# Projections to the merge gates read their tokens with a step of 2, 4, 8 or 16

## The chip, the core and the metric

The kernel runs on one core of a Trainium2 chip, as one launch. The metric is device time in microseconds from the start to the end of one execution. A profiled execution also gives the span from its first to its last instruction and a record of every instruction on the five engines: PE (TensorE, with its weight loads PEld), DVE (VectorE), ACT (ScalarE), POOL (GpSimd) and SP (SyncE).

## The reference

512 tokens of width 2048 go through two blocks in float32. The part that the change touches is the first block's pair of merge gates, `g_att` and `g_ssm`, each 2048 wide:

```
h = rms_norm(x, ln_gain)                      # 512 x 2048
proj = h @ w_in                               # 512 x 10240
q, k, v, z_att, u, z_ssm, g_att, g_ssm = split(proj)
...                                           # attention on q, k, v; a grouped state-space branch on u
merged = sigmoid(g_att) * (y_att @ w_proj_att) + sigmoid(g_ssm) * (y_ssm @ w_proj_ssm)
x = x + merged @ w_out
```

The second block (two layers of three kinds of attention, each with its projections and a gate) follows and is not touched.

## The kernel before

Activations are held transposed: features on the 128 partitions, the 512 tokens along each partition. The normalised input is 16 tiles `xg`, one per 128 features, of shape 128 x 2 x 512: a high half rounded to fp32r and a low half with the remainder, so that a product takes three fp32r matmuls (`mm3`, L180: high by high, high by low, low by high) that add up in PSUM. Weights come from memory in units of 128 x 1024 (`wunit`, L192), are split in the same way by ACT (L189) and DVE (L190), and wait in three buffers `hl`.

`gemm_t` (L224) makes a product in the transposed layout: the weights are stationary (128 x 128), the tokens stream as the moving operand, 512 columns in a row, and two PSUM tiles `pg` of 128 x 512 are filled over the 16 feature tiles. That is 2 x 16 x 3 = 96 matmuls of 512 columns in one call. PSUM has four `pg` buffers, so that one call's two tiles can be emptied during the next call.

`accumulate` (L246) walks the matmuls of a call, and after each group of three calls `tick`, which takes steps of other work that were pushed beside it. This sets the order: while the gates are computed, the steps of the state-space branch (`ssm`, L482) lie between the groups of three. Among these steps are small fp32 matmuls: L549 (16 columns), L557 and L584 (64 columns side by side), and L586, whose moving operand is `st[:, :64, g0 + q + g]` of a tile of 65 x 64 elements, so 64 columns that stand 64 elements (256 bytes) apart. An fp32 matmul is two records in the trace.

The gates are the loop at L638 to L645: 16 calls of `gemm_t`, eight for `g_att` (columns from GA0) and eight for `g_ssm` (from GS0). After each call, for each of its two PSUM tiles, DVE multiplies by the row `row` of inverse norms into a tile `t` (L643), ACT takes the sigmoid in place (L644), and POOL issues the store to the scratch `sg_d` (L645). Later, at L689 and L690, these are loaded as the merge needs them.

Three DVE operations elsewhere use steps along a partition: L629 reads PSUM and `row` with a step of 8 elements (32 bytes), L559 writes `st` with a step of 64, L708 writes with a step of 8.

Of the kernel before, what the change touches and what calls it, by code (L numbers as in the profile page):

```python
# [17 lines left out]
T = 512  # L18
# [9 lines left out]
Q0, K0, V0, ZA0, U0, ZS0, GA0, GS0 = 0, 1024, 2048, 3072, 4096, 5120, 6144, 8192  # L28
# [89 lines left out]
class Net:  # L118
# [102 lines left out]
                pass  # L221
        self.between = []

    def gemm_t(self, src, c0, mov, n=T):  # L224

        out = [self.psg()[:, :n] for _ in range(2)]

        def step(hl, k, kk, i, first, last):
            x = mov[k]
            c = slice(i * P, (i + 1) * P)  # L230
            self.mm3(out[i], hl[:, 0, kk, c], hl[:, 1, kk, c], x[:, 0], x[:, 1], first, last)

        return self.accumulate(src, c0, len(mov), out, step, AT_MEM if n == NMEM else AT_T)

    def gemm_tok(self, src, c0, mov, nt, cw=256):

        out = [self.psg()[:, :cw] for _ in range(nt)]

        def step(hl, k, kk, i, first, last):
            x = mov[k]  # L240
            t = slice(i * P, (i + 1) * P)
            self.mm3(out[i], x[:, 0, t], x[:, 1, t], hl[:, 0, kk], hl[:, 1, kk], first, last)

        return self.accumulate(src, c0, len(mov), out, step, AT_TOK if cw == 256 else AT_T, cw)
# [350 lines left out]
    def first(self):  # L595
        nc, tc, a = self.nc, self.tc, self.a
        v = nc.vector
        w_in = a["w_in"]
# [8 lines left out]
        with ExitStack() as sx:  # L607
            xp = sx.enter_context(tc.tile_pool(name="xg1", bufs=KD, reuse_waits="tile"))
            xg = []
            by_chunk = "p (m j) -> p j m"  # L610
            with ExitStack() as ix:
                stage = ix.enter_context(tc.tile_pool(name="ins", bufs=2, side="right", reuse_waits="tile"))
                mx = ix.enter_context(tc.tile_pool(name="memx", bufs=KD, side="right", reuse_waits="tile"))
                acc = self.new_acc()
                for _ in self.transposed_in(a["x"], 4, xp, xg, self.ln_g, stage, acc, spill=self.xt_d):
                    pass
                row, cols = self.norm_stats(acc)
                self.row, self.cols = row, cols
                self.more_columns()
                mem, acc = [], stage.tile([P, 512], F32, name="macc", bufs=1)[:, :NMEM]  # L620
                for f in range(0, 8, 2):
                    if f == 4:
                        self.push(self.transposed_in(a["mem"], 2, mx, mem, self.mem_g, stage, acc), MEM_IN_EVERY)
                    us = self.gemm_t(w_in, U0 + f * P, xg)
                    self.ahead = AHEAD
                    for i, ps in enumerate(us):
                        t = self.t512()
                        with self.soon():
                            v.tensor_mul(t.rearrange("p (j m) -> p j m", j=8), ps.rearrange(by_chunk, j=8),  # L629
                                         row.rearrange(by_chunk, j=8))  # L630
                        self.store(self.u_d[(f + i) * P:(f + i + 1) * P], t)
                self.flush()
                self.rpb_windows()
                self.memory_kv(mem, *self.norm_stats(acc, NMEM, stage))
            with tc.tile_pool(name="ssm", bufs=3, side="right", reuse_waits="tile") as sp:

                self.push(self.ssm(sp), SSM_EVERY)
                work = [(c0 + f * P, self.sg_d[s], f) for s, c0 in enumerate((GA0, GS0)) for f in range(0, KD, 2)]  # L638
                for c0, dst, f in work:
                    for i, ps in enumerate(self.gemm_t(w_in, c0, xg)):  # L640
                        t = self.t512()
                        with self.soon():
                            v.tensor_mul(t, ps, row)  # L643
                        nc.scalar.activation(t, t, AF.Sigmoid)  # L644
                        self.store(dst[(f + i) * P:(f + i + 1) * P], t)  # L645
                self.ssm_gates(xg, 0)
                self.flush()
            with tc.tile_pool(name="glu", bufs=8, side="right", reuse_waits="tile") as gp:
                yt, yh = [], []
                self.push(self.ssm_out(gp, yt, yh), GELU_EVERY)  # L650
                self.ssm_gates(xg, 4)
                self.flush()
                for f in range(0, 8, 2):
                    for i, ps in enumerate(self.gemm_t(a["w_glu"], f * P, yh)):
                        t, z = self.t512(), self.t512()
                        r = slice((f + i) * P, (f + i + 1) * P)
                        self.load(z, self.zs_d[r])
                        last = nc.scalar.activation(t, ps, AF.Sigmoid, bias=self.b_glu[:, f + i:f + i + 1])
                        v.tensor_mul(t, t, yt[f + i])
                        v.tensor_mul(z.rearrange(by_chunk, j=8), z.rearrange(by_chunk, j=8),  # L660
                                     t.rearrange("p (j m) -> p j m", j=8))
                        self.store(self.ys_d[r], z)
            self.exp_tables(last)
            with tc.tile_pool(name="att1", bufs=2, side="right", reuse_waits="tile") as ap:
                self.causal = ap.tile([P, 512], F32, name="causal", bufs=1)
                self.load(self.causal, a["causal"])
                for h in range(0, 8, 2):
                    self.diff_heads(ap, h, xg)
                self.flush()
            yp = tc.alloc_tile_pool(name="y1", bufs=16, side="right", reuse_waits="tile")  # L670
            ya, ys = [], []
            for f in range(0, 8, 2):
                for i, ps in enumerate(self.gemm_t(w_in, ZA0 + f * P, xg)):
                    ya.append(self.gated(yp, ps, f + i))
            for f in range(8):
                t = self.t512()
                self.load(t, self.ys_d[f * P:(f + 1) * P])
                h = yp.tile([P, 2, 512], FR, tag="yh", name=self.nm("yh"))
                self.split(h[:, 0], h[:, 1], t)
                ys.append(h)  # L680
        mp = tc.alloc_tile_pool(name="mrg", bufs=KD, side="left", reuse_waits="tile")
        mg = []
        for f in range(0, KD, 2):
            pa = self.gemm_t(a["w_proj_att"], f * P, ya)
            pb = self.gemm_t(a["w_proj_ssm"], f * P, ys)
            for i in range(2):
                r = slice((f + i) * P, (f + i + 1) * P)
                t, u = self.t512(), self.t512()
# [6 lines left out]
                h = mp.tile([P, 2, 512], FR, tag="m", name=self.nm("m"))  # L695
# [4 lines left out]
        xg, acc = [], self.new_acc()  # L700
        self.x1_d = dram.tile([D, T], F32, name="x1_d")
        for f in range(0, KD, 2):
            for i, ps in enumerate(self.gemm_t(a["w_out"], f * P, mg)):
                k = f + i
                r = slice(k * P, (k + 1) * P)
                t, o = self.t512(), self.t512()
# [569 lines left out]
```

## Time and profile before

| | us |
|---|---|
| two runs, median (lowest to highest) | 3308.08 (3307.55 to 3308.61) |
| the profiled execution, whole | 3310.56 |
| its span, first to last instruction | 3308.7 |
| PE busy in the span | 3272.4 (99%) |
| DVE busy | 1749.5 (53%) |
| ACT busy | 1168.2 (35%) |
| first to last L643 (emptying of the gates' tiles) | 231.4 to 630.5 |

The profile gives each engine's busy time, the span in 40 slices with the clock that TensorE was granted, the chain of work that ended last, and groups of instructions by source line with durations and the idle time before them. Matmuls overlap: a record's duration is longer than the distance to the next matmul's start, and its end is modelled. So the pace of PE is read from the starts in a timeline, and what a column costs from the difference of durations between shapes.

### The profile page before, as it was taken

To read this page: it belongs to the slowest core of one execution; us is meant where nothing else is said; L and a number is where in the kernel's file an instruction comes from. 1 tells how busy PE (TensorE), PEld (TensorE's weight loads), DVE (VectorE), ACT (ScalarE), POOL (GpSimd) and SP (SyncE) were. 2 spreads that over 40 slices of the span, in tenths; PEclk is the share of its full clock that TensorE was granted. 3 is DMA by queue.
4 is the path that set the end of the run, shared out by engine and by line. 5 is a ranking of instruction groups with operands and counts; after the bars stand their busy time and mean duration, and the time that the engine had idled before them with its cause. 6 is when DMAs were issued, how large, how long until landed. Compare 5 with 4: busy or idle time off the path is not lost.

```text
span 3308.7 us, 43728 instructions
## 1 busy us (share of the span) xinstructions
PE 3272.4 (99%) x17268; PEld 2794.0 (84%) x17268; DVE 1749.5 (53%) x3207; ACT 1168.2 (35%) x1811; POOL 292.9 (9%) x426
## 2 busy tenths in 40 slices
PE   8999999999999999999999999999999999999998
PEld 6998877888888788888888888888888888888788
DVE  5464486445888754434444556443354445554333
ACT  4432222243555432233333334323333333343322
POOL 3200001311111000011011000001100100000000
PEclk9999999999999999999999999999999999999999
DMA  6564443453333354344333222334443222223433
GB/s 222 181 199 120 128 124 120 136 188 134 98 101 99 109 183 151 124 142 154 96 95 100 90 83 80 121 118 143 147 135 100 95 90 90 83 93 121 144 120 102
DMA packets 359805, 410.03 MB, mean 124 GB/s; under 512 B 36506, under 2 KB 314921, under 8 KB 359472
## 3 DMA queue, kind: packets, MB, share of 16 engines
q1 hardware_dynamic: 344656, 363.73, 34.5%
q0 software_dynamic: 14944, 43.52, 3.7%
q8 instruction: 135, 2.21, 0.3%
q14 instruction: 70, 0.57, 0.1%
HBM read 355.86 MB, written 47.70 MB: 122 GB/s over the span
## 4 chain that ended last, share of the span: by engine, by line
PE 95%; DVE 3%; issue 1%; DMA 1%; ACT 0%; POOL 0%; SPq 0%; ACTq 0%; DVEq 0%; POOLq 0%
PE pg L183 29%; PE pg L185 28%; PE pg L184 28%; PE pa L1140 1%; PE pa L184 1%; PE pa L185 1%; PE pa L183 1%; DVE hl L190 1%; PE pa L586 0%; DVE s L568 0%; DVE st L570 0%; DVE s L567 0%; DVE s L569 0%; DMA in<-in_x_dram 0%; DVE s L566 0%
## 5 line engine op out<-in xcount | busy, mean ns | idle before, releaser
L190 DVE TENSOR_TENSOR hl<-raw,hl 128x1024 fp32r<-128x1024 f32 x552 | 681.7, 1236 | 951.4 <-ACT hl L189 949.8
L183 PE MATMUL pg<-xg,hl 128*128 128x512 f32 (+1 forms) x2688 | 1068.2, 397 | 0.0
L185 PE MATMUL pg<-xg,hl 128*128 128x512 f32 (+1 forms) x2688 | 1038.2, 386 | 8.9 <-DVE hl L190 8.9
L184 PE MATMUL pg<-xg,hl 128*128 128x512 f32 (+1 forms) x2688 | 1037.1, 386 | 0.0
L189 ACT CAST hl<-raw 128x1024 fp32r<-128x1024 f32 x552 | 579.1, 1050 | 1099.1 <-PE pg L185 928.4
L185 PEld LDWEIGHTS pg<-xg,hl 128*128 128x128 f32 x2688 | 505.2, 188 | 115.5 <-DVE hl L190 13.9
L183 PEld LDWEIGHTS pg<-xg,hl 128*128 128x128 f32 x2688 | 506.8, 189 | 88.3 <-DVE v L315 0.9
L184 PEld LDWEIGHTS pg<-xg,hl 128*128 128x128 f32 x2688 | 507.2, 189 | 80.6
L183 PE MATMUL pg<-hl,xg 128*128 128x256 f32 x1152 | 326.7, 284 | 0.0
L185 PE MATMUL pg<-hl,xg 128*128 128x256 f32 x1152 | 321.6, 279 | 0.0
L184 PE MATMUL pg<-hl,xg 128*128 128x256 f32 x1152 | 321.6, 279 | 0.0
L183 PE MATMUL pg<-yh,hl 128*128 128x512 f32 x576 | 224.1, 389 | 0.0
L184 PE MATMUL pg<-yh,hl 128*128 128x512 f32 x576 | 224.1, 389 | 0.0
L185 PE MATMUL pg<-yh,hl 128*128 128x512 f32 x576 | 224.1, 389 | 0.0
L185 PEld LDWEIGHTS pg<-hl,xg 128*128 128x128 f32 x1152 | 218.7, 190 | 0.0
L183 PEld LDWEIGHTS pg<-hl,xg 128*128 128x128 f32 x1152 | 216.8, 188 | 1.5
L184 PEld LDWEIGHTS pg<-hl,xg 128*128 128x128 f32 x1152 | 216.6, 188 | 1.6
L190 DVE TENSOR_TENSOR wt<-pa,wt 128x512 fp32r<-128x512 f32 (+3 forms) x144 | 83.1, 577 | 118.2 <-ACT wt L189 117.7
L189 ACT CAST wt<-pa 128x512 fp32r<-128x512 f32 (+3 forms) x144 | 71.3, 495 | 166.5 <-PE pa L1140 166.0
L183 PEld LDWEIGHTS pg<-yh,hl 128*128 128x128 f32 x576 | 108.1, 188 | 22.6
L185 PEld LDWEIGHTS pg<-yh,hl 128*128 128x128 f32 x576 | 108.1, 188 | 22.6
L184 PEld LDWEIGHTS pg<-yh,hl 128*128 128x128 f32 x576 | 108.1, 188 | 22.1
(283 smaller groups left out, 3867.3 us busy)
## 6 DMA issues: line engine op xcount, KB each, us to landing
raw<-in_w_in_dram SPq DMA_DIRECT2D x384, 512.0 KB, 3.5
raw<-in_w_out_dram SPq DMA_DIRECT2D x96, 512.0 KB, 3.3
raw<-in_w_mem_kv_dram SPq DMA_DIRECT2D x32, 512.0 KB, 4.4
o_d<-t POOLq DMA_DIRECT2D x40, 256.0 KB, 2.3
t<-o_d SPq DMA_DIRECT2D x40, 256.0 KB, 3.9
sg_d<-t POOLq DMA_DIRECT2D x32, 256.0 KB, 2.5
raw<-in_w_proj_att_dram SPq DMA_DIRECT2D x16, 512.0 KB, 3.6
raw<-in_w_proj_ssm_dram SPq DMA_DIRECT2D x16, 512.0 KB, 3.2
```

What stands on the lines that cost most here:

```text
L183: mm(ps, wh, xh, start=start, stop=False)
L184: mm(ps, wh, xl, start=False, stop=False)
L185: mm(ps, wl, xh, start=False, stop=stop)
L189: self.nc.scalar.copy(hi, src)
L190: self.nc.vector.tensor_sub(lo, src, hi.bitcast(F32))
L1140: self.nc.tensor.transpose(pt[:, i * P:(i + 1) * P], w, self.ident)
```

## The change

`gemm_t` gets a parameter `every`. Where it is over 1, the moving operand's view takes the tokens j, j + n, j + 2n and so on for j = 0 to n - 1, so that consecutive columns stand n elements apart, and the PSUM tile is filled contiguously in that order. The gates' loop passes n = 2 for the first four calls of `g_att`, 4 for its other four, 8 for the first four of `g_ssm` and 16 for the last four: 8, 16, 32 and 64 bytes between columns. The multiplication at the evacuation reads PSUM contiguously, and reads `row` and writes `t` with step n, which puts the tokens in natural order again. The built program has the same instructions in the same order on every engine; the shapes of the 32 DVE multiplications (128x512 becomes 128 x n x 512/n) and the access patterns of 1536 matmuls differ.

```diff
-    def gemm_t(self, src, c0, mov, n=T):
+    def gemm_t(self, src, c0, mov, n=T, every=1):
...
         def step(hl, k, kk, i, first, last):
-            x = mov[k]
+            x, o = mov[k], out[i]
+            if every > 1:
+                x = x.rearrange("p h (m j) -> p h j m", j=every)
+                o = o.rearrange("p (j m) -> p j m", j=every)
             c = slice(i * P, (i + 1) * P)
-            self.mm3(out[i], hl[:, 0, kk, c], hl[:, 1, kk, c], x[:, 0], x[:, 1], first, last)
+            self.mm3(o, hl[:, 0, kk, c], hl[:, 1, kk, c], x[:, 0], x[:, 1], first, last)
...
                 for c0, dst, f in work:
-                    for i, ps in enumerate(self.gemm_t(w_in, c0, xg)):
+                    n = 2 ** (1 + f // 8 + 2 * (c0 >= GS0))
+                    for i, ps in enumerate(self.gemm_t(w_in, c0, xg, every=n)):
                         t = self.t512()
                         with self.soon():
-                            v.tensor_mul(t, ps, row)
+                            v.tensor_mul(t.rearrange("p (m j) -> p j m", j=n), ps.rearrange("p (j m) -> p j m", j=n),
+                                         row.rearrange("p (m j) -> p j m", j=n))
```

## Rows read from the trace of the kernel before

**Rows 1.** The page's busy times, granted clock by slice, and chain by engine.
```profile
PE 3272.4 (99%) x17268; PEld 2794.0 (84%) x17268; DVE 1749.5 (53%) x3207; ACT 1168.2 (35%) x1811; POOL 292.9 (9%) x426
PEclk9999999999999999999999999999999999999999
...
PE 95%; DVE 3%; issue 1%; DMA 1%; ACT 0%; POOL 0%; SPq 0%; ACTq 0%; DVEq 0%; POOLq 0%
```

**Rows 2.** Busy time by stretch of the gates' stage; then PE's waits, 211 to 632.
```profile
core 0: us, PE busy (x) PEld busy (x) DVE busy (x) ACT busy (x) POOL busy (x), PEclk, DMA share, GB/s
270.00:330.00 60.00, 60.00 (x323) 50.55 (x322) 23.82 (x42) 13.31 (x18) 3.23 (x6) 1.00 0.39 116
420.00:541.00 121.00, 112.07 (x487) 89.55 (x486) 106.95 (x369) 25.98 (x30) 7.73 (x12) 1.00 0.40 127
541.00:632.00 91.00, 91.00 (x492) 78.18 (x491) 39.98 (x78) 21.09 (x26) 26.78 (x46) 1.00 0.43 131
...
PE pg L185 <- DVE hl L190: 8.9, 10, 1.1
```

**Rows 3.** Timeline of PE in the gates' stage: start us, us, what.
```profile
229.20 0.39 PE L183 MATMUL pg<-xg,hl 128*128 128x512 f32 x1
229.43 0.39 PE L184 MATMUL pg<-xg,hl 128*128 128x512 f32 x1
229.65 0.39 PE L185 MATMUL pg<-xg,hl 128*128 128x512 f32 x1
229.88 0.39 PE L183 MATMUL pg<-xg,hl 128*128 128x512 f32 x1
```

**Rows 4.** By line, fp32r of 512 contiguous columns: duration ns min/median/max, first and last start.
```profile
L183 PE MATMUL pg<-yh,hl x576: 389/389/389, 725.9 to 2407.7; 128*128 128x512 f32 x192
```

**Rows 5.** By line, fp32 matmuls of 1, 512, 64 and 64 strided columns.
```profile
L289 PE MATMUL pa<-onesD,acc x24: 165/250/250, 54.6 to 2418.1; 128*128 128x1 f32 x24
L284 PE MATMUL pa<-acc,onesD x6: 590/593/697, 53.6 to 2417.0; 128*128 128x512 f32 x6
L584 PE MATMUL pa<-u,dm x128: 217/264/275, 548.0 to 665.9; 128*128 128x64 f32 x128
L586 PE MATMUL pa<-st,f x128: 270/288/312, 549.0 to 666.2; 128*128 128x64 f32 x128
```

**Rows 6.** By line, DVE: contiguous (L643, L339) and with a step (L629, L708, L559).
```profile
L643 DVE TENSOR_TENSOR t<-pg,rstd x32: 676/691/692, 231.4 to 630.5; 128x512 f32<-128x512 f32 x32
L629 DVE TENSOR_TENSOR t<-pg,rstd x8: 1106/1136/1172, 62.0 to 120.7; 128x512 f32<-128x512 f32 x8
L708 DVE TENSOR_TENSOR t<-t,pg x16: 1122/1130/1139, 1375.7 to 1533.0; 128x512 f32<-128x512 f32 x16
L339 DVE COPY t<-pa x16: 673/681/692, 13.2 to 51.8; 128x512 f32<-128x512 f32 x16
L559 DVE COPY st<-pa x8: 1059/1069/1087, 289.7 to 424.0; 128x512 f32<-128x512 f32 x8
```

## The prediction, before the changed kernel ran

> **What bounds the kernel.** [...] Then the gates' stage by stretches: PE has no idle time in two of the three stretches shown, and in the third, where DVE is busy 107 of 121 us, it lacks 9 us; its only waits there are 8.9 us for the weights' low halves [rows 2]. So whatever a matmul of this stage takes longer comes out at the end, one for one. The timeline gives the pace: starts at 229.20, 229.43, 229.65, 229.88, so 0.227 us for each matmul of 512 columns [rows 3].
>
> **What the change touches.** The instructions and their order stay. 16 calls x 96 matmuls = 1536 matmuls get a moving operand with a step, 384 for each of 8, 16, 32 and 64 bytes. 32 DVE multiplications get a step. Weight loads, DMAs and stores stay as they are.
>
> **What a column with a step costs on PE.** No fp32r matmul here has a step. One line has it with fp32: L586, 64 columns that stand 256 bytes apart. Its shortest record is 270 ns, that of L584, with the same shape side by side, 217 ns, and a matmul of one column takes 165 ns [rows 5]. I take the shortest because the second of a matmul's two records also holds a wait for its weights. So a contiguous fp32 column takes (217 - 165) / 64 = 0.81 ns, over 512 columns (593 - 165) / 512 = 0.84 ns, and a strided one (270 - 165) / 64 = 1.64 ns: twice as long. The granted clock is 1.00 in that stretch [rows 2]. The read of the moving operand does limit PE when columns lie far apart.
>
> [...]
> - [...] DVE shows a like price: L629, with a step of 32 bytes, takes 1136 ns against 691 for L643 on contiguous data, (1136 - 691) / 512 = 0.87 ns more for each element; L559 against L339 0.76 ns; L708 against L643 0.86 ns [rows 6]. A DVE element with a step thus takes nearly 2 ns, a time of the same size as PE's 1.64 ns.
> [...]
>
> [...] The matmul streams 512 columns in 389 - 165 = 224 ns now.
> - Steps of 16, 32 and 64 bytes: 512 x 1.67 = 855 ns, 631 ns more, x 1152 = **+727 us**. [...]
> - Step of 8 bytes: two columns share a fetch, 512 x 0.835 = 428 ns, 204 ns more, x 384 = **+78 us**. [...]
> - PE's waits for weights: a slower PE gives DVE and ACT more time for each unit, so the 8.9 us go: **-9 us** at most.
> - DVE: L643 goes from 691 to about 1136 ns (L629's row), 0.44 us more, 32 x 0.44 = 14 us of DVE time. Two of the four PSUM tiles are emptied while PE fills the other two for 96 x 0.227 = 22 us, and this takes 2.3 us, so PE does not see it. Without that cover it would cost 14 us. ACT's sigmoid and POOL's store start 0.4 us later and nobody needs them before the merge.
> - Weight loads (0.19 us) stay hidden behind longer matmuls. The small matmuls between the groups, L586 included, are unchanged.
>
> Sum: 3310.6 (the profiled execution, 2.5 us or 0.08% over the median of the two runs, which I neglect) + 727 + 78 - 9 = **4107 us**. With 1.64 ns it is 3310.6 + 709 + 75 - 9 = 4086, with 1.75 ns 3310.6 + 774 + 86 - 9 = 4162.
>
> [...]
>
> **Rivals.**
> [...]
> 2. *Half rate.* [...] For it: L586's exact factor of two. [...] With 0.84 ns (204 ns more) 1152 x 0.204 = 235: 3310.6 + 235 - 9 = 3537 us; with 0.82 ns (196 ns more) 3527, and if then a step of 16 bytes pays only half of its share, 38 us less, 3490.
> 3. *Half rate at every step*, 8 bytes too: 3537 + 78 = 3615 us.
> 4. *Not slower: these steps are read at full pace.* [...] PE then keeps 0.227 us a matmul and DVE's 14 us are hidden: 3302 to 3311 us. For it: L586 is the only strided row on PE, at another step and another type. Against it: DVE pays as much at 32 bytes (L708) as at 256 (L559). The point from which it decides: 2% of the time is 66 us, 43 ns on each of 1536 matmuls, so it holds if starts stay under 0.27 us apart.
> [...]
>
> **Numbers.** Forecast 0.36, rival 1 0.13, rival 2 0.27, rival 3 0.06, rival 4 0.11, others 0.07. The range goes from 3490 (rival 2 with its lower bound) to 4170 (forecast at 1.75 ns); it leaves out rival 4 and a part of the others. The forecast's own range is 4080 to 4165. Differences below 2%, 66 us, count as no change: that is rival 4. Slower by over 2% are all other cases; nothing here removes work that could make it faster by as much, beyond what is unknown.
>
> **What the changed profile would show.** Starts of matmuls in the gates' stage, quarter by quarter: 0.43, 0.86, 0.86 and 0.86 us if the forecast holds, 0.23 and then 0.86 by rival 1, 0.23 and then 0.43 by rival 2, 0.43 throughout by rival 3, 0.23 throughout by rival 4. The multiplication at the evacuation should take about 1.13 us at 32 bytes, with no wait of PE for it. The granted clock should stay at 1.00, and the rest of the span, before 211 us and after the gates, should keep its length; if it does not, the sum lacks a term. The forecast is wrong if the last three quarters differ among themselves by more than a tenth, or if the fp32 record of L586, which is unchanged, no longer shows 270 ns.

## The result and the profile after

The changed kernel takes **3624.7 us** (median of two runs, 3624.03 to 3625.38) against 3308.08: a ratio of 1.095 [1.0935, 1.097], 317 us more. The forecast was 4107 us, 799 us more. The direction was right, the size was not: the forecast's own range was 4080 to 4165 us.

The page of the changed kernel, its span, busy times, granted clock by slice and chain by engine, answers to [rows 1]:

```profile
span 3623.6 us, 43728 instructions
...
PE 3596.6 (99%) x17268; PEld 2823.8 (78%) x17268; DVE 1759.2 (49%) x3207; ACT 1171.2 (32%) x1811; POOL 291.8 (8%) x426
PEclk9999999999999999999999999999999999999999
...
PE 98%; DMA 1%; ACT 0%; DVE 0%; issue 0%; POOL 0%; SPq 0%; ACTq 0%; DVEq 0%; POOLq 0%
```

PE bounds the kernel as before (99% busy, 98% of the chain) and the granted clock stays at 0.9 or more in every slice (mean 0.998 before, 0.999 now). PE's busy time grew by 324 us, the span by 315, DVE's by 10: all of it is PE's.

The gates' stage by the quarters in which the steps are 2, 4, 8 and 16, with the columns of [rows 2] (stretch, then PE, PEld, DVE, ACT and POOL busy, clock, DMA share, GB/s):

```profile
211.00:394.00 183.00, 183.00 (x477) 88.24 (x476) 63.96 (x144) 27.97 (x37) 5.37 (x10) 1.00 0.27 79
394.00:594.00 200.00, 200.00 (x608) 103.53 (x607) 48.20 (x75) 27.82 (x37) 8.01 (x13) 1.00 0.23 70
594.00:760.00 166.00, 166.00 (x388) 79.27 (x387) 103.87 (x360) 21.82 (x25) 6.40 (x10) 1.00 0.24 76
760.00:946.00 186.00, 186.00 (x568) 99.57 (x568) 48.76 (x85) 24.92 (x30) 29.75 (x52) 1.00 0.25 76
```

The stage is 735 us long. Before it lay between 211 and 631 us, 420 us, in quarters of 98, 114, 108 and 100 us. The difference, 315 us, is the whole difference of the spans. PE has no idle time in any quarter now. The third and fourth quarters aren't cut at quite the same place of the program (431 and 527 matmuls before, 388 and 568 now), so they are best read together.

The timeline of PE, two starts from each quarter (start, us, what), answers to [rows 3]:

```profile
225.69 0.63 PE L183 MATMUL pg<-xg,hl 128*128 128x512 f32 x1
226.14 0.63 PE L184 MATMUL pg<-xg,hl 128*128 128x512 f32 x1
...
452.26 0.66 PE L184 MATMUL pg<-xg,hl 128*128 128x512 f32 x1
452.72 0.66 PE L185 MATMUL pg<-xg,hl 128*128 128x512 f32 x1
...
699.87 0.61 PE L183 MATMUL pg<-xg,hl 128*128 128x512 f32 x1
700.30 0.61 PE L184 MATMUL pg<-xg,hl 128*128 128x512 f32 x1
...
909.57 0.61 PE L183 MATMUL pg<-xg,hl 128*128 128x512 f32 x1
910.00 0.62 PE L184 MATMUL pg<-xg,hl 128*128 128x512 f32 x1
```

| quarter, step | start to start, us | forecast | more than 0.227 | x 384 |
|---|---|---|---|---|
| 1: 2 tokens, 8 bytes | 0.451 to 0.455 | 0.43 | 0.225 | 86 us |
| 2: 4 tokens, 16 bytes | 0.460 to 0.462 | 0.86 | 0.234 | 90 us |
| 3: 8 tokens, 32 bytes | 0.431 | 0.86 | 0.204 | 78 us |
| 4: 16 tokens, 64 bytes | 0.433 | 0.86 | 0.206 | 79 us |

The starts account for 333 us, and the stage grew by 315. Of the 18 us between them 8.9 us are the waits of [rows 2], of which the changed kernel has none in this stage. The other 9 us lie around the small fp32 matmuls. Two starts behind one of them, first before, then now:

```profile
390.33 0.48 PE L183 MATMUL pg<-xg,hl 128*128 128x512 f32 x1
390.65 0.39 PE L184 MATMUL pg<-xg,hl 128*128 128x512 f32 x1
...
453.25 0.70 PE L183 MATMUL pg<-xg,hl 128*128 128x512 f32 x1
453.76 0.66 PE L184 MATMUL pg<-xg,hl 128*128 128x512 f32 x1
```

Before, the first fp32r matmul behind a small one took 0.315 us to the next start, 0.09 more than the others' 0.227; now it takes 0.04 to 0.05 more than the others of its quarter. The stage has 266 of these, so that is some 10 us less. The small matmuls' own starts lie further apart now (two of them take 0.156 to 0.158 us up to the next fp32r start, before 0.138 to 0.140), 5 us the other way, and the rest is scattered.

The other rows that the prediction named, by line (count, duration in ns as min/median/max, first and last start): the multiplication at the evacuation, L648 now, with steps of 8 and of 32 bytes, and the fp32 matmul with 64 strided columns, L590 now:

```profile
L648 DVE TENSOR_TENSOR t<-pg,rstd x8: 691/692/693, 247.7 to 393.7; 128x512 f32<-128x512 f32 x8
...
L648 DVE TENSOR_TENSOR t<-pg,rstd x9: 1125/1130/1216, 593.6 to 759.6; 128x512 f32<-128x512 f32 x9
...
L590 PE MATMUL pa<-st,f x128: 272/288/311, 810.3 to 981.0; 128*128 128x64 f32 x128
```

L590's shortest record is where it was, 272 against 270 ns [rows 5]. DVE pays nothing at 8 bytes (692 ns against 691) and 0.44 us at 32 (1130), the size of [rows 6].

### The profile page after: what moved, and what is told of

Its sections match the earlier page's. It is cut to its first block, busy times and chain, and to the rows that moved or that the text cites. A ratio compares the mean times of both kernels' runs of the same rounds, so it can differ in the third digit from the quotient of the medians.

```text
span 3623.6 us, 43728 instructions
## 1 busy us (share of the span) xinstructions
PE 3596.6 (99%) x17268; PEld 2823.8 (78%) x17268; DVE 1759.2 (49%) x3207; ACT 1171.2 (32%) x1811; POOL 291.8 (8%) x426
## 4 chain that ended last, share of the span: by engine, by line
PE 98%; DMA 1%; ACT 0%; DVE 0%; issue 0%; POOL 0%; SPq 0%; ACTq 0%; DVEq 0%; POOLq 0%
PE pg L183 30%; PE pg L184 30%; PE pg L185 30%; PE pa L1146 1%; PE pa L184 1%; PE pa L185 1%; PE pa L183 1%; PE pa L590 0%; PE pa L787 0%; PE pa L588 0%; DMA in<-in_x_dram 0%; PE pa L561 0%; PE pa L857 0%; PE pa L856 0%; DMA raw<-in_w_mem_kv_dram 0%
## 5 line engine op out<-in xcount | busy, mean ns | idle before, releaser
L183 PE MATMUL pg<-xg,hl 128*128 128x512 f32 (+1 forms) x2688 | 1178.4, 438 | 0.0
L185 PE MATMUL pg<-xg,hl 128*128 128x512 f32 (+1 forms) x2688 | 1157.2, 430 | 0.5 <-DVE hl L190 0.5
L184 PE MATMUL pg<-xg,hl 128*128 128x512 f32 (+1 forms) x2688 | 1157.4, 431 | 0.0
L185 PEld LDWEIGHTS pg<-xg,hl 128*128 128x128 f32 x2688 | 514.7, 191 | 200.5 <-issue 117.4
L183 PEld LDWEIGHTS pg<-xg,hl 128*128 128x128 f32 x2688 | 512.5, 191 | 149.0 <-issue 75.7
L184 PEld LDWEIGHTS pg<-xg,hl 128*128 128x128 f32 x2688 | 511.5, 190 | 128.2 <-issue 57.5
```

The source lines that it names most:

```text
L183: mm(ps, wh, xh, start=start, stop=False)
L184: mm(ps, wh, xl, start=False, stop=False)
L185: mm(ps, wl, xh, start=False, stop=stop)
```

## The experiments

Every kernel ran beside the kernel before on the same chip, whose time stands in brackets; where an interval is given the kernel ran several times, else the time is that of one execution. Only the gates' stage differs unless said. An fp32r matmul's pace is read from the starts; 16 calls of 96 matmuls make the stage.

### Runs of 2, 4 and 8 neighbours: is it the step, or how many neighbours stand together?

The columns come in runs of r neighbours, and a run starts 8r elements after the one before: r = 2, 4, 8 in the first three quarters; in the last r = 2 again, one element off the 8-byte boundary. The evacuation is viewed in the same way.

```diff
-            x = mov[k]
+            x, o = mov[k], out[i]
...
+                if odd:
+                    x = x.rearrange("p h t -> p (h t)")
+                    x = [x[:, q:q + T].rearrange("p (m j i) -> p j m i", j=j, i=r) for q in (1, T - 1)]
+                else:
+                    x = [x[:, q].rearrange("p (m j i) -> p j m i", j=j, i=r) for q in range(2)]
...
+                    n = ((8, 2, 0), (8, 4, 0), (8, 8, 0), (8, 2, 1))[f // 8 + 2 * (c0 >= GS0)]
```

> The tokens are read in runs of neighbours with jumps between the runs: first quarter of the gates runs of 2 tokens (8 bytes), second of 4, third of 8, last runs of 2 that begin 4 bytes off an 8-byte boundary (there the tokens are shifted by one, so the gates' values are moved by a token). [...] Theory B (any pattern that is not one contiguous stream goes at half pace): 0.43 in all quarters, about 3625. [...]

Measured: 3467.97 us (3309.97). The timeline of this kernel, two starts from the first, second and fourth quarters:

```profile
270.00 0.61 PE L185 MATMUL pg<-xg,hl 128*128 128x512 f32 x1
270.43 0.61 PE L183 MATMUL pg<-xg,hl 128*128 128x512 f32 x1
...
466.72 0.41 PE L184 MATMUL pg<-xg,hl 128*128 128x512 f32 x1
466.97 0.41 PE L185 MATMUL pg<-xg,hl 128*128 128x512 f32 x1
...
635.28 0.61 PE L183 MATMUL pg<-xg,hl 128*128 128x512 f32 x1
635.71 0.61 PE L184 MATMUL pg<-xg,hl 128*128 128x512 f32 x1
```

Runs of 2 cost 0.431 us, the same as steps of 8 and 16 without any neighbours, on and off the boundary. Runs of 4 cost 0.244 to 0.250, runs of 8 0.233 (starts at 545.07 and 545.30) in the first half of their quarter and 0.25 to 0.27 in the second (586.31, 586.57, 586.85), for which no row gives a reason. In this arrangement two neighbours side by side are worth nothing to fp32r (0.431 us), four nearly everything (0.244 to 0.250, against 0.227 contiguous). Theory B, 0.43 us in all quarters, falls with the second and the third. That four neighbours are always needed isn't so either: the run on places below has 0.231 us with two.

### Steps from 1 to 128, fp32r

One call for each step 1, 2, 4, ... 128, and then back to 1, so that each step comes at two places of the stage. Theory A of the expectation is that every step from 2 on costs what the changed kernel's four steps cost. The edit is against the changed kernel.

```diff
-                    n = 2 ** (1 + f // 8 + 2 * (c0 >= GS0))
+                    call = f // 2 + 8 * (c0 >= GS0)
+                    n = 2 ** (call if call < 8 else 15 - call)
```

> The sixteen calls of the gates get steps of 1, 2, 4, 8, 16, 32, 64, 128 and then 128 down to 1 elements, so each step stands in two places of the stage. Theory A: 0.23 us at step 1, 0.43 to 0.46 at every other step up to 512 bytes; about 3309 + 1344 x 0.205 = 3585 us. [...] On the extra 0.02 to 0.03 us that steps 2 and 4 showed over 8 and 16 in the changed kernel: if it belongs to the step, it shows in both places of the stage; if it belongs to the place (the side work there), it goes with the place.

Measured: 3557.67 us (3309.97). Starts by step: 1: 0.227; 2: 0.452; 4: 0.461; 8: 0.431; 16 and 32: 0.433; 64: 0.487; 128: 0.272 to 0.283 us. Three of them in the timeline, steps 128, 64 and 16:

```profile
560.12 0.45 PE L184 MATMUL pg<-xg,hl 128*128 128x512 f32 x1
560.41 0.45 PE L185 MATMUL pg<-xg,hl 128*128 128x512 f32 x1
...
600.24 0.67 PE L183 MATMUL pg<-xg,hl 128*128 128x512 f32 x1
600.72 0.67 PE L184 MATMUL pg<-xg,hl 128*128 128x512 f32 x1
...
689.90 0.61 PE L183 MATMUL pg<-xg,hl 128*128 128x512 f32 x1
690.33 0.61 PE L184 MATMUL pg<-xg,hl 128*128 128x512 f32 x1
```

The extra of steps 2 and 4 goes with the step, at both places alike. Nobody expected the largest step to be cheap. At step 128 the reading goes round four places, 512 bytes apart, and comes back to each of them at the next element. So the price doesn't go by the distance from one column to the next alone (0.487 us at 256 bytes, 0.272 to 0.283 at 512); why, no row shows.

### The same steps in fp32

The same kernel, with one fp32 matmul of the high halves in place of the three fp32r ones.

```diff
-            self.mm3(o, hl[:, 0, kk, c], hl[:, 1, kk, c], x[:, 0], x[:, 1], first, last)
+            if every:
+                self.nc.tensor.matmul(o, hl[:, 0, kk, c].bitcast(F32), x[:, 0].bitcast(F32), start=first, stop=last)
```

> The gates' products are made of the high halves alone, as one fp32 matmul (two records) in place of three fp32r ones; steps as in the sweep, 1 to 128 elements and back. [...]

Measured: 3728.34 us (3309.97), though it makes one product where there were three: its time says little, its records do. Start to start, for each of a matmul's two records: step 1 0.429, 2 0.450, 4 0.900, 8 0.918, 16 0.858, 32 0.861, 64 0.863, 128 0.873 us. By line and stretch (a record's duration is some 0.17 us longer than the distance of the starts), steps 1, 2, 4 and 16:

```profile
L236 PE MATMUL pg<-xg,hl x38: 590/601/648, 1019.5 to 1039.8; 128*128 128x512 f32 x38
...
L236 PE MATMUL pg<-xg,hl x35: 609/612/612, 244.6 to 259.9; 128*128 128x512 f32 x35
...
L236 PE MATMUL pg<-xg,hl x36: 1076/1078/1096, 924.4 to 959.5; 128*128 128x512 f32 x36
...
L236 PE MATMUL pg<-xg,hl x19: 1034/1034/1035, 834.1 to 849.5; 128*128 128x512 f32 x19
```

In fp32 a column does cost 1.68 to 1.8 ns at every step from 4 on (858 to 918 / 512), close to the 1.64 ns estimated from L586 [rows 5], and at step 2 only 0.88 ns (450 / 512), next to 0.84 at step 1 (429 / 512). The forecast's 428 ns at 8 bytes and 855 from 16 bytes on, made for fp32r, are near what fp32 takes.

### The evacuation alone

PE reads contiguously; DVE keeps the steps of the changed kernel (the gates' tokens then come out in another order). The edit is against the changed kernel; it ran once, and then several times.

```diff
-                    for i, ps in enumerate(self.gemm_t(w_in, c0, xg, every=n)):
+                    for i, ps in enumerate(self.gemm_t(w_in, c0, xg)):
```

> TensorE reads contiguous tokens as before, and only the multiplications at the evacuation keep their steps (the gates' tokens come out in another order). If they are hidden: 3308 us, with 0.69 us at step 2 and 1.03 to 1.15 us at the others for each. If they hold PSUM tiles back from TensorE: up to 14 us more, 3322. The whole 316 us should be absent.

> The multiplications at the evacuation alone keep their steps, once more and timed. One look gave 4 us more than before, and the waits of TensorE for the weights' low halves on VectorE grew from 8.9 to 12.8 us. If that is the price: 3312 to 3315 us, 0.1%. If it was chance: no difference.

Measured: 3314.23 (3309.97), and in the several runs 3313.64 against 3309.52 us, ratio 1.0015 [1.0006, 1.0025]: 4 us. PE's waits in the gates' stage of this kernel (engine, line, what it waited for; us, times, longest):

```profile
PE pg L185 <- DVE hl L190: 12.7, 11, 1.6
...
PE pa L548 <- DVE e L483: 1.2, 2, 1.0
```

The waits are 13.9 us in place of 8.9. PE never waits for the emptied tiles; what it waits for is DVE's other work, the low halves of the weights (12.7 us, before 8.9) and the scan (1.2 us, before none). So 4 of the 317 us could be the evacuation's with PE at its old pace, and with PE slowed there is no wait left to see. The rest comes with the moving operand's step.

### Where the columns lie, with the same number of neighbours

Four patterns, one to a quarter (`every` is its number); the evacuation is contiguous. Quarter 1: step 256, so two places in turn. Quarters 2 and 3 read the same elements, two of every four: in 2 the columns alternate between two places half of the data apart, so that the first and second neighbour of a place come two columns apart; in 3 the neighbours stand side by side. Quarter 4: as 2, with four places.

```diff
+            if every == 1:
+                x = x.rearrange("p h (m j) -> p h j m", j=256)
+                x, o = (x[:, 0], x[:, 1]), o.rearrange("p (j m) -> p j m", j=256)
+            elif every:
+                x, q = x.rearrange("p h t -> p (h t)"), 4 if every == 4 else 2
+                if every == 3:
+                    x = x.rearrange("p (q m z) -> p m q z", q=q, z=4)
+                    x, o = (x[:, :, :, :2], x[:, :, :, 2:]), o.rearrange("p (m q z) -> p m q z", q=q, z=2)
+                else:
+                    x = x.rearrange("p (q m z) -> p m z q", q=q, z=4)
+                    x, o = (x[:, :, :2], x[:, :, 2:]), o.rearrange("p (m z q) -> p m z q", q=q, z=2)
```

> The gates read tokens that do not make up the gates (their values are meaningless, and the evacuation is contiguous); only the pace is of interest. Quarter 1: step 256, columns from two places in turn, each place then read neighbour by neighbour. Quarter 2: two places 512 elements apart in turn, two neighbours from each (0, 512, 1, 513, 4, 516, 5, 517, ...). Quarter 3: the same elements with the neighbours side by side (0, 1, 512, 513, 4, 5, 516, 517, ...). Quarter 4: four places 256 apart in turn, two neighbours from each. [...]

Measured: 3438.59 us (3309.52). The timeline, quarter by quarter:

```profile
245.04 0.38 PE L184 MATMUL pg<-xg,hl 128*128 128x512 f32 x1
245.25 0.38 PE L185 MATMUL pg<-xg,hl 128*128 128x512 f32 x1
...
345.45 0.40 PE L184 MATMUL pg<-xg,hl 128*128 128x512 f32 x1
345.68 0.40 PE L185 MATMUL pg<-xg,hl 128*128 128x512 f32 x1
...
490.95 0.67 PE L184 MATMUL pg<-xg,hl 128*128 128x512 f32 x1
491.43 0.67 PE L185 MATMUL pg<-xg,hl 128*128 128x512 f32 x1
...
630.36 0.51 PE L184 MATMUL pg<-xg,hl 128*128 128x512 f32 x1
630.68 0.51 PE L185 MATMUL pg<-xg,hl 128*128 128x512 f32 x1
```

The moving operands of quarters 2 and 3 differ in nothing but the order of the columns, 0.231 against 0.48 to 0.51 us. So for fp32r the order alone makes a factor of two, and neighbours cost less with a column of the other place between them than side by side. Quarter 1 takes 0.216 us for 512 columns, less than the contiguous 0.227 of the kernel before, and quarter 4 takes 0.328 us. No row shows what in the read makes these differences.

### The same places in fp32

The edit is against the run on places.

```diff
-            self.mm3(o, hl[:, 0, kk, c], hl[:, 1, kk, c], x[0], x[1], first, last)
+            if every:
+                self.nc.tensor.matmul(o, hl[:, 0, kk, c].bitcast(F32), x[0].bitcast(F32), start=first, stop=last)
```

> The patterns of the run on places, read by fp32 matmuls: the gates' products are made of one fp32 matmul of the high halves (two records) in place of three fp32r ones, and the tokens read do not make up the gates. Quarter 1: columns from two places in turn (0, 256, 1, 257, ...). Quarter 2: two places in turn, two neighbours from each (0, 512, 1, 513, 4, 516, ...). Quarter 3: the same with the neighbours side by side (0, 1, 512, 513, 4, 5, ...). Quarter 4: four places in turn, two neighbours from each. [...]

Measured: 3597.12 us (3308.09). By line and stretch, the four quarters:

```profile
L246 PE MATMUL pg<-xg,hl x30: 703/703/703, 259.3 to 275.0; 128*128 128x512 f32 x30
...
L246 PE MATMUL pg<-xg,hl x28: 814/823/890, 419.5 to 439.3; 128*128 128x512 f32 x28
...
L246 PE MATMUL pg<-xg,hl x43: 642/642/642, 589.6 to 609.7; 128*128 128x512 f32 x43
...
L246 PE MATMUL pg<-xg,hl x24: 1061/1061/1061, 699.4 to 719.7; 128*128 128x512 f32 x24
```

Start to start this is 0.540, 0.655, 0.480 and 0.883 us. With two places in turn fp32 (0.540 and 0.655) lies between its 0.429 us at step 1 and its 0.858 to 0.918 at steps from 4 on. The order of quarters 2 and 3 is turned round: side by side is the quicker in fp32 (0.480 against 0.655), the slower in fp32r (0.48 to 0.51 against 0.231). And fp32 with two places, 0.540 and 0.655, takes about twice what fp32r takes with four, 0.272 to 0.283 (step 128, above) and 0.328. These are measured paces; no row gives their reason.

### Weights with a step

The stationary operand is read with steps of 1, 2, 4, 8 by quarter, the tokens contiguously.

```diff
+                w = [v.rearrange("p (m j) -> p j m", j=every)[:, 0, at // every:at // every + P] if every < 8 else
+                     v.rearrange("p (m j) -> p j m", j=8)[:, i] for v in w]
```

> The tokens are contiguous again, and the stationary operand has the step: the 128 columns of a weight load stand 1, 2, 4 and 8 elements apart in the four quarters (other weights than the gates', so their values are meaningless). [...] If the price is only the moving read's: 188 ns and 0.227 us throughout, about 3310 us.

Measured: 3326.01 us (3309.52). The weight loads by line and stretch, steps 1, 4 and 8:

```profile
L184 PEld LDWEIGHTS pg<-xg,hl x14: 187/188/192, 245.5 to 254.7; 128*128 128x128 f32 x14
...
L184 PEld LDWEIGHTS pg<-xg,hl x29: 308/309/311, 459.9 to 479.6; 128*128 128x128 f32 x29
...
L184 PEld LDWEIGHTS pg<-xg,hl x16: 329/332/332, 532.7 to 544.4; 128*128 128x128 f32 x16
```

With step 2 they take 196 ns. A step of 16 bytes costs a load about 0.12 us (309 ns against 188), 8 bytes next to nothing, like fp32 (0.450 us against 0.429) and DVE (692 ns against 691). Though a load then takes longer than a matmul's 0.227 us, starts lie only 0.23 to 0.247 us apart between fp32r matmuls: there most of the price is hidden. Behind a small fp32 matmul it is not: at step 8 the first fp32r matmul's record lasts 612 ns, against 476 before, and some 75 of these make 10 of the 16 us by which the kernel is longer.

### The change's job in runs of four

Tokens in the order of a step, but in runs of 4 neighbours, 16 bytes (j = 8, i = 4) in all calls, put in natural order at the evacuation.

```diff
+                    x = [x[:, q].rearrange("p (m j i) -> p j m i", j=j, i=r) for q in range(2)]
...
+                    n = (8, 4, 0)
...
+                            by = dict(j=n[0], i=n[1])
+                            v.tensor_mul(t.rearrange("p (m j i) -> p j m i", **by), ps.rearrange("p (j m i) -> p j m i", **by),
+                                         row.rearrange("p (m j i) -> p j m i", **by))
```

> All gates read their tokens in runs of four neighbours (16 bytes) that stand 32 tokens apart, put in natural order at the evacuation: the same thing as the change does, but with whole lines. [...]

Measured: 3324.56 against 3309.52 us, ratio 1.0046 [1.0031, 1.0061]; starts are 0.247 us apart (470.21, 470.46, 470.71), as with runs of 4 in the first experiment (0.244 to 0.250). It is 300 us under the changed kernel.

### Two places in turn, for the gates and for every product of this kind

The columns alternate between token m and token m + 256, PSUM is filled in that order and read with step 2 where it is emptied: first in the gates alone, then in all calls of `gemm_t` with 512 tokens but those for `u`, with each consumer's view adapted (the edit below is of the second). This is the pattern of quarter 1 of the run on places; theory P of the two expectations carries its pace there, 0.216 us, over to all these matmuls.

```diff
+def two(ap):
+    return ap.rearrange("p (j m) -> p j m", j=2)
...
             x = mov[k]
+            if pair:
+                x = x.rearrange("p h (j m) -> p h m j", j=2)
...
+                o = out[i].rearrange("p (m j) -> p m j", j=2)
...
+        return [o.rearrange("p (m j) -> p j m", j=2) for o in out] if pair else out
...
-                            v.tensor_mul(t, ps, row)
+                            v.tensor_mul(two(t), ps, two(row))
```

> [...] The evacuation reads PSUM with a step of 2 and writes contiguously. The quarter with this pattern ran at 0.216 us a matmul in the run on places, against 0.227 contiguous. Theory P: 0.216 throughout the gates, 0.69 us for each multiplication (step 2 cost VectorE nothing in the changed kernel): up to 1536 x 0.011 = 17 us less, 3292; less of it where VectorE is late in the scan. If the quick quarter owed its pace to something else there: 3309.

> The same pattern in all products of 512 tokens that gemm_t makes, but for the four calls of u: 9792 matmuls in place of 1536, every evacuation reading PSUM with a step of 2. Theory P: 9792 x 0.011 = 108 us less, 3202 us, if no other engine becomes the limit; the reads of PSUM with a step of 2 (8 bytes) should cost VectorE and ScalarE nothing, as in the changed kernel's first quarter. If they do cost 0.4 us each, some of it is hidden and the gain shrinks by up to 40 us.

Measured: 3295.42 us for the gates alone (3309.36), and for all **3204.21 against 3309.36 us**, ratio 0.968 [0.9662, 0.9694]. The page of the kernel with all, and starts in its timeline from a product outside the gates:

```profile
span 3202.2 us, 43752 instructions
...
PE 3160.1 (99%) x17268; PEld 2805.2 (88%) x17268; DVE 1748.4 (55%) x3207; ACT 1165.2 (36%) x1811; POOL 291.4 (9%) x426
```

```profile
1249.87 0.38 PE L189 MATMUL pg<-yh,hl 128*128 128x512 f32 x1
1250.09 0.38 PE L187 MATMUL pg<-yh,hl 128*128 128x512 f32 x1
```

9792 matmuls of 0.216 in place of 0.227 us would give 108 us; measured are 105. PE's busy time is 112 us under [rows 1], with as many instructions. The evacuations pay nothing for the step of 8 bytes in PSUM: 688 ns against 691 for the gates' multiplication. This version beats both kernels.

## Why the prediction was wrong, point by point

- **What bounds the kernel** was right: PE has no slack in the stage, and what a matmul takes longer came out at the end. DVE's price (0.44 us at 32 bytes) was right and hidden. So were the clock (1.00) and the rest of the span. The waits for weights are gone, as forecast, and 9 us more with them, around the small fp32 matmuls.
- **The failed step** is the price of a column in the term for 16, 32 and 64 bytes: 1.67 ns, twice the 0.84 ns of a contiguous fp32 column and near the 1.64 estimated from L586. It was taken from fp32 and applied to fp32r. In fp32 it is borne out: 1.68 to 1.8 ns a column at every step from 4 on, 0.88 at step 2. No run shows it for fp32r, nor the 1.75 ns at the upper end of the forecast's range; there the runs show 0.84 to 0.90 ns a column (0.431 to 0.462 us / 512). The term, 631 ns a matmul and 727 us, was 0.204 to 0.234 us and 247 us by the starts. That is 480 of the 482 us by which the forecast was too high; the waits, the 8-byte term and the time of the profiled execution make up the rest.
- **The term for 8 bytes** was about right, 78 us forecast, 86 measured, and that was luck: the term has two columns share a fetch, which no run shows. What the runs show for fp32r is that this step costs as much as the others (0.451 to 0.455 us, against 0.431 to 0.462).
- **The rival with the nearest number**, half rate at every step (3615 us, chance 0.06), came near all four starts with 0.43 us throughout (its sum takes 204 ns more for a matmul where 0.84 ns a column gives 206, 2 us in all). Its price, 0.84 ns a column, is that of contiguous fp32 (0.429 us / 512); fp32r pays 0.84 to 0.90 at steps from 2 to 32 (0.431 to 0.462 us) and 0.84 for runs of 2 (0.431), but not for two places in turn (0.216 and 0.231 us). At steps of 4 to 32 fp32 takes about twice as long (0.858 to 0.918), at step 2 as long (0.450 against 0.452). Why fp32r falls to this pace, the times don't show.
- **Contiguous fp32r** is not quite twice as fast as fp32: 0.44 against 0.84 ns a column [rows 4, 5], 5% more than half. Reading two places in turn is 5% quicker (0.216 against 0.227 us); no row says why.
- **The prediction's own signs of being wrong** did not show: the last three quarters differ by 7%, under the tenth that it allowed, and L586's shortest record stayed where it was (272 against 270 ns). What told was the size of the starts.

The step could have been seen as weak: the price came from one fp32 row and was carried to fp32r, which takes a column every 0.44 ns. Half of that price at all four steps stood among the rivals, with a chance of 0.06.

## What to carry to other kernels

A price per column that is read from one type has to be measured in the type to which it is applied, before it is multiplied by a thousand matmuls. If tokens have to be reordered, keep runs of four fp32 neighbours (16 bytes) in an fp32r moving operand (0.247 in place of 0.43 to 0.46 us here), or do it at the evacuation, where 8-byte steps were free (692 ns against 691) and all steps together cost 4 us. Where PE bounds a kernel with contiguous fp32r operands, try reading two halves of the row in turn: here it was worth 5% on each matmul (0.216 against 0.227 us) and 3.2% of the whole time (3204 against 3309 us).

## What was not expected, and what stays open

- Step 256 is faster than no step (0.216 against 0.227 us for 512 columns), and step 128 costs only 0.272 to 0.283 us, while step 64 costs 0.487, more than 8 to 32.
- Steps 2 and 4 cost 0.02 to 0.03 us more than 8 and 16 in fp32r; in fp32 it is 4 and 8 that cost more (0.900 and 0.918 against 0.858). No run explains this, nor the 0.48 to 0.51 us of pairs side by side in two places against 0.431 for runs of 2 at a smaller distance.
- What several places read in turn cost is known at single points only (0.272 to 0.283 and 0.328 us with four places in fp32r, 0.540 and 0.655 with two in fp32).
- Runs of 8 neighbours took 0.233 us in one half of their quarter and 0.25 to 0.27 in the other, with 2 us of waits in the whole stage.
